# Forming the low halves of the split weights with an accumulating DMA instead of a VectorE subtraction

## The chip, the cores and the metric

The kernel runs on one core of a Trainium2 chip. The metric is the time of one execution on the device in microseconds (us); the times of a kernel are given as the median of several runs. Five engines work side by side, each through its own instructions in order: TensorE (PE, matrix products; PEld is its weight loads), VectorE (DVE), ScalarE (ACT), GpSimd (POOL) and SyncE (SP, which here only issues transfers). Sixteen DMA engines move data between the device memory (HBM) and the on-chip memory (SBUF); a transfer is issued by one of the engines' queues and is moved by all sixteen.

## The reference

Two decoder layers over a sequence of 512 positions with 1024 channels, in float32. Layer 0 mixes by windowed pooling and block-sparse attention, layer 1 by a gated recurrence (RG-LRU); each is followed by a gated feed-forward block with a short convolution.

```python
h = rms_norm(x, norm_mix[l])
x = x + (pool_attn_mixer(h, ...) if l % 2 == 0 else rglru_mixer(h, ...))
h = rms_norm(x, norm_ffn[l])
x = x + conv_ffn(h, ffn_w_in[l], ffn_conv_w[l], ffn_conv_b[l], ffn_w_out[l])
# rglru_mixer: z = h @ w_in; gate, xr = split(z); xr = causal_dwconv(xr)
# r, i = sigmoid of two 128x128 block products of xr;  a = exp(-8 r softplus(-lam))
# b = sqrt(1 - a^2) * (i * xr);  hs = scan(a, b);  out = (gelu(gate) * hs) @ w_out
```

All products are computed to nearly float32 precision. TensorE multiplies a rounded type (float32r), so each operand is split into a high part (rounded) and a low part (what the rounding left), and a product is three: high·high, high·low, low·high.

## The kernel before

Activations are kept with channels on the 128 partitions and the 512 positions along the free axis. The weights stream through in 218 chunks of up to 128x1024 float32 (512 KB), 99.1 MB in all, in the order in which TensorE uses them: 8 chunks of the query and key projections, 17 more of the first mixer, 76 of the first feed-forward block, 41 of the recurrence, 76 of the second feed-forward block. A feed-forward block is done in two halves of 22 up chunks (24 products of 512 columns each: the tiles `up`) and 16 down chunks (18 or 15 products: `dn`). The recurrence has 20 chunks of its input projection (`xr` for the branch, `gt` for the gate), 5 small chunks of 128x512 for the gate products (`gp`; each serves two of the ten blocks), then 16 down chunks.

A chunk passes three steps. SP loads it into a raw buffer (`wraw`, three of them, line 182). ACT rounds it into the high part (`whi`, line 195). DVE subtracts the high part from the raw one into the low part (`wlo`, line 196). The five gate chunks use their own buffers, `shi` and `slo`, of which there is one each; all others rotate through four pairs `whi`/`wlo`. `wnext` keeps three chunks converted ahead of the one in use, so chunk i takes the buffers of chunk i-4, and its conversion can begin when TensorE has read chunk i-4 for the last time. A gate chunk can be converted only when the products of the gate chunk before it are done.

`mm3` (lines 217 to 220) issues the three products in the order high·high, high·low of the activation, low·high: the low part of a chunk is first read by its third product (in the token projections, where the weights are the moving operand, by the second).

A scheduler lays out each engine's instructions from the program and its dependences; in parts of the program (`pe["on"]`: the first mixer and the recurrence) TensorE's order is fixed by hand. In the recurrence, `RG_ORDER` lists the steps: branch tile (x), gate products (p), gate tile (g), exponentials (e), square roots (q), scan (s), gelu (o), product (y). A step s has three instructions in a chain: DVE forms `h` (line 770), POOL multiplies it by `yy` (line 771), DVE scans (line 772). The five scans of a batch come one after the other. POOL otherwise does little: the sums of squares `ss` of the norms (line 260), the window sums of the pooling, and the product `yy<-i,a` (line 813).

Of the kernel before, what the change touches and what calls it, by code (L numbers as in the profile page):

```python
# [14 lines left out]
ALU = mybir.AluOpType  # L15
# [23 lines left out]
    _n += _w  # L39
NPA = _n  # L40

# Order of the first mixer: u/f = pooled projection now / as filler between attention steps, c = centre a window sum,
# v = value projection, m = split a pooled tile, a = attention.
MIX_ORDER = "u3 c3 u2 v m m f1 f0 a".split()
# Fillers of the attention loop: u = next projection group, m = split, p = pooled product, o = output product.
FILL_ORDER = "uuuuuuuuuuuuuuuuupmmpopp"
POOL_ORDER = (3, 2, 1, 0)
FILL_RATES = [float(c) for c in "1.6 1.95 1.45".split()]
# [8 lines left out]
CENTRE_AT = 5  # L57
V_BANKS = ("mm", "mm", "s", "av")
WARM = 20
# Order of the RG-LRU: x = branch tile, p = its gate products, g = gate tile, e = exps, q = roots, s = scan, o = gelu,  # L60
# y = output tile.
RG_ORDER = []
_c = dict.fromkeys("xpgeqsoy", 0)
for _kind in "xxgxpxpqxpgpgpeqsxsxxsssopyooxpxypygpgpqesssoosygsogyyogoyyggooyy":
    RG_ORDER.append((_kind, _c[_kind]))
    _c[_kind] += 1
RAW, WB, AHEAD = 3, 4, 3


@with_exitstack  # L70
def tile_trunk(ctx: ExitStack, tc: tile.TileContext, xT, par, fpar, w_v, w_q, w_k, w_u, w_pool, w_po, w_ao,
               f0_in, f0_out, r_in, r_ax, r_out, f1_in, f1_out, out):
    nc = tc.nc
# [7 lines left out]
    def T(tag, dt=F32):  # L81
        return cur["tp"].tile([P, S], dt, name=tag, tag=tag, bufs=cur["bufs"][tag])

    def phase(name, **bufs):
        if "cm" in cur:
            cur["cm"].__exit__(None, None, None)
        cur["cm"] = tc.tile_pool(name=name, bufs=1)
        cur["tp"] = cur["cm"].__enter__()
        cur["bufs"] = bufs
# [23 lines left out]
    def f(t):  # L113
        return t.bitcast(F32)
# [20 lines left out]
    chunks = []  # L135
# [31 lines left out]
    ready = []  # L167
# [7 lines left out]
    def load(parts=1):  # L175
        src, n = chunks[len(raws)]
        raw = wp.tile([P, 1024], F32, name="wraw", bufs=RAW)[:, :n]
        for i in range(parts):
            c = slice(i * n // parts, (i + 1) * n // parts)
            nc.sync.dma_start(raw[:, c], src[:, c])  # L180
        raws.append(raw)

    def convert():
        n = chunks[len(ready)][1]
        if len(raws) == len(ready):
            load()
        raw = raws[len(ready)]
        if n == S and "shi" in cur["bufs"]:
            hi, lo = T("shi", F32R), T("slo", F32R)
        else:  # L190
            hi, lo = (wp.tile([P, 1024], F32R, name=t, bufs=WB)[:, :n] for t in ("whi", "wlo"))
        parts = 2 if len(ready) < 2 else 2 if pe["on"] and len(ready) in FINE else 1
        for i in range(parts):
            c = slice(i * n // parts, (i + 1) * n // parts)
            nc.scalar.copy(hi[:, c], raw[:, c])  # L195
            nc.vector.tensor_tensor(lo[:, c], raw[:, c], f(hi[:, c]), op=ALU.subtract)  # L196
        ready.append((hi, lo, n))

    def wnext(n, ahead=AHEAD):
        while len(ready) < min(used[0] + 1 + ahead, len(chunks)):  # L200
            convert()
        hi, lo, got = ready[used[0]]
        assert got == n
        used[0] += 1
        return hi, lo
# [109 lines left out]
            if len(spans) == 1:  # L315
                after(d)

# [1 line left out]
    phase("mix0", qka=20, pm=4, hn=5, bias=1, lg=4)  # L319
    psum("ps0", mm=3, s=2, tr=2, av=1)  # L320
    warm = onesr.bitcast(BF16)
# [356 lines left out]
        g()  # L678
    ring[:] = ["mm", "s", "mm", "s", "mm", "av"]

# [1 line left out]
    def ffn(layer, norm, after, cuts=None):  # L682
        def conv(m):
            c0 = (layer * 2 * NF + m) * 4
            cw = [fprm[:, c0 + i:c0 + i + 1] for i in range(4)]
            ps = up_tile(norm, "up")
            bc = norm.bc
            z = T("z")
            nc.vector.tensor_tensor(z, ps, bc, op=ALU.mult)  # L689
            a = T("a")  # L690
            nc.scalar.activation(a, z, AF.Identity, scale=cw[2], bias=cw[3])  # L691
            for sh, w in ((1, cw[1]), (2, cw[0])):
                nc.vector.scalar_tensor_tensor(a[:, sh:], z[:, :S - sh], w, a[:, sh:], op0=ALU.mult, op1=ALU.add)  # L693
            return a

        for h0 in range(2):
            half(h0 * NF // 2, conv, after if h0 else (lambda d: None), cuts if h0 else None)
# [17 lines left out]
    n1 = Norm("nm1")  # L715
    ffn(0, nf, n1.tile_done)

# [1 line left out]
    phase("mix1", z=2, a=3, xrs=6, i=2, h=10, gz=6, shi=1, slo=1, yy=20)  # L719
    lam = prm[:, PC["lam"]:PC["lam"] + RB]  # L720
    sc = [cst.tile([P, RB], F32, name=f"sc{i}") for i in range(5)]
# [19 lines left out]
    now = {"set": "", "last": None, "before": None, "conv": None}  # L741
# [10 lines left out]
    for kind, n in RG_ORDER:  # L752
# [29 lines left out]
        if kind == "x":  # L782
# [5 lines left out]
            a = T("a")  # L788
# [6 lines left out]
            hi, lo = T("xrs", F32R), T("xrs", F32R)  # L795
# [4 lines left out]
        a, xh, xl = XC[n]  # L800
# [3 lines left out]
        for s in range(2):  # L804
            c = slice((2 * (n % 2) + s) * P, (2 * (n % 2) + s + 1) * P)
            gp = PS("gp", "tr")
            mm3(gp, gwh[:, c], gwl[:, c], xh, xl, True, True)
            o = T("yy" if s == 0 else "i")
# [87 lines left out]
```

## Time and profile before

| | |
|---|---|
| median of 3 runs | 1108.43 us (1108.22 to 1109.06) |
| span of the profiled execution | 1106.8 us |
| PE busy | 1091.4 us, 99% |
| DVE busy | 726.8 us, 66% |
| ACT busy | 514.6 us, 46% |
| POOL busy | 89.7 us, 8% |
| DMA, mean | 95 GB/s |

The span runs from the first instruction to the last on the device; the median of the runs is 1.6 us longer than it. TensorE is busy nearly throughout, but matmuls overlap: each is shown with 389 ns, while one begins every 227 ns in a steady stretch, so a chunk of 24 products takes 5.44 us, and a busy share alone does not tell a stall. Stalls are read from the starts of the matmuls and from the bracket with the idle time in the timeline.

### The profile page before, as it was taken

The page shows a single profiled execution, that of the slowest core. Times are in us where ns is not written, and L with a number is a line of the kernel's source. Part 1 is how long each engine was busy: PE and PEld are TensorE (multiplying, and loading weights), DVE is VectorE, ACT ScalarE, POOL GpSimd, SP SyncE. Part 2 cuts the span into 40 slices and gives each one's busy share as a digit, 9 for nine tenths or more (in the row PEclk, how much of TensorE's full clock was granted, in tenths as well). Part 3 has the DMA queues.
Part 4 walks back from the last instruction along what each step waited for, and adds up shares of the span by engine and source line. Part 5 has one row for each costly group of instructions (what it writes and reads, how often), then busy time and mean ns, then how long its engine had stood idle before and what let it go on. Part 6 is the DMA issues. An engine that isn't in the chain of part 4 may idle for free.

```text
span 1106.8 us, 12775 instructions
## 1 busy us (share of the span) xinstructions
PE 1091.4 (99%) x4895; PEld 893.2 (81%) x4895; DVE 726.8 (66%) x1013; ACT 514.6 (46%) x749; POOL 89.7 (8%) x70
## 2 busy tenths in 40 slices
PE   8999999999999999999999899999999999999998
PEld 6887778888888888888888687788888888888887
DVE  7777867877753477764486979448777435777631
ACT  6556656544432344444458695444444323444320
POOL 4030002100000000000202323120000000000000
PEclk9999999999999999999999999999999999999999
DMA  6332112222223322223332131342322243332241
GB/s 223 129 95 87 58 39 71 102 95 96 72 82 111 117 96 98 94 73 91 113 113 105 48 101 48 99 136 95 102 97 78 79 119 116 96 95 84 72 137 51
DMA packets 35261, 105.40 MB, mean 95 GB/s; under 512 B 4096, under 2 KB 4992, under 8 KB 35200
## 3 DMA queue, kind: packets, MB, share of 16 engines
q1 hardware_dynamic: 34416, 103.48, 28.7%
q10 hardware_dynamic: 784, 1.11, 0.4%
q8 instruction: 38, 0.62, 0.2%
q14 instruction: 23, 0.19, 0.1%
HBM read 101.43 MB, written 2.10 MB: 94 GB/s over the span
## 4 chain that ended last, share of the span: by engine, by line
PE 90%; DVE 6%; ACT 2%; issue 1%; DMA 0%; POOL 0%; SPq 0%; DVEq 0%; POOLq 0%; ACTq 0%
PE up L218 43%; PE dn L218 26%; PE tk L218 5%; PE xr L218 2%; PE gt L218 2%; PE po L218 2%; PE u L218 2%; PE ao L218 2%; DVE h L772 1%; PE s L218 1%; DVE wlo L196 1%; PE tr L221 1%; PE gp L218 1%; DVE a L791 1%; DVE h L770 1%
## 5 line engine op out<-in xcount | busy, mean ns | idle before, releaser
L195 ACT CAST whi<-wraw 128x1024 fp32r<-128x1024 f32 (+3 forms) x225 | 202.5, 904 | 281.0 <-PE dn L218 154.2
L196 DVE TENSOR_TENSOR wlo<-wraw,whi 128x1024 fp32r<-128x1024 f32 (+3 forms) x225 | 238.9, 1065 | 114.2 <-ACT whi L195 111.6
L218 PE MATMUL up<-xl,whi 128*128 128x512 f32 x704 | 274.0, 389 | 0.0
L218 PE MATMUL up<-xh,whi 128*128 128x512 f32 x704 | 273.9, 389 | 0.0
L218 PE MATMUL up<-xh,wlo 128*128 128x512 f32 x704 | 273.9, 389 | 0.0
L218 PE MATMUL dn<-yy,whi 128*128 128x512 f32 (+1 forms) x886 | 269.2, 386 | 2.4 <-ACT yy L230 2.0
L218 PEld LDWEIGHTS dn<-yy,whi 128*128 128x128 f32 x886 | 165.8, 189 | 36.9 <-ACT yy L230 2.8
L218 PE MATMUL dn<-yy,wlo 128*128 128x512 f32 (+1 forms) x443 | 170.7, 385 | 0.0
L218 PEld LDWEIGHTS up<-xl,whi 128*128 128x128 f32 x704 | 132.2, 188 | 27.9 <-DVE xl L234 0.5
L218 PEld LDWEIGHTS up<-xh,whi 128*128 128x128 f32 x704 | 132.2, 188 | 27.4
L218 PEld LDWEIGHTS up<-xh,wlo 128*128 128x128 f32 x704 | 132.2, 188 | 27.2
L693 DVE SCALAR_TENSOR_TENSOR a<-z,fprm,a 128x510 f32<-128x510 f32 (+1 forms) x176 | 131.1, 748 | 4.2 <-ACT a L691 1.1
L689 DVE TENSOR_TENSOR z<-up,rbc 128x512 f32<-128x512 f32 x88 | 60.5, 688 | 89.1 <-PE up L218 89.1
L218 PEld LDWEIGHTS dn<-yy,wlo 128*128 128x128 f32 x443 | 83.6, 189 | 16.4
L260 POOL TENSOR_TENSOR ss<-ss,sq 128x512 f32<-128x512 f32 x28 | 41.3, 1475 | 494.1 <-ACT sq L259 493.6
L230 ACT CAST yy<-y 128x512 fp32r<-128x512 f32 x44 | 27.3, 621 | 112.1 <-DVE y L707 112.1
L312 DVE TENSOR_TENSOR x<-dn,x 128x512 f32<-128x512 f32 (+1 forms) x41 | 27.8, 679 | 73.9 <-PE dn L218 73.9
L691 ACT ACTIVATE a<-z,fprm 128x512 f32<-128x512 f32 x88 | 71.4, 814 | 3.8 <-DVE z L689 3.2
L704 ACT ACTIVATE gg<-a 128x512 f32<-128x512 f32 x44 | 27.8, 632 | 81.1 <-DVE a L693 81.0
L231 DVE TENSOR_TENSOR yy<-y,yy 128x512 fp32r<-128x512 f32 x44 | 30.5, 692 | 28.9 <-ACT yy L230 28.9
L218 PE MATMUL tk<-wlo,xh 128*128 128x512 f32 x96 | 37.7, 392 | 1.9 <-DVE wlo L196 1.9
L218 PE MATMUL tk<-whi,xh 128*128 128x512 f32 x96 | 37.9, 400 | 1.2 <-ACT whi L195 1.2
(177 smaller groups left out, 1229.5 us busy)
## 6 DMA issues: line engine op xcount, KB each, us to landing
wraw<-in_dram SPq DMA_DIRECT2D x131, 512.0 KB, 3.3
wraw<-in_dram SPq DMA_DIRECT2D x48, 320.0 KB, 2.8
wraw<-in_dram SPq DMA_DIRECT2D x32, 384.0 KB, 3.0
x<-in_dram SPq DMA_DIRECT2D x8, 256.0 KB, 5.9
out_dram<-x SPq DMA_DIRECT2D x7, 256.0 KB, 2.0
wraw<-in_dram SPq DMA_DIRECT2D x6, 256.0 KB, 2.7
qka<-qka ACTq DMA_DIRECT2D x8, 128.0 KB, 2.6
wraw<-in_dram SPq DMA_DIRECT2D x4, 128.0 KB, 3.8
```

The costliest lines, as they stand in the source:

```text
L195: nc.scalar.copy(hi[:, c], raw[:, c])
L196: nc.vector.tensor_tensor(lo[:, c], raw[:, c], f(hi[:, c]), op=ALU.subtract)
L218: in_order(nc.tensor.matmul(*a, **k))
L221: in_order(nc.tensor.transpose(*a))
L230: nc.scalar.copy(hi, src)
L231: nc.vector.tensor_sub(lo, src, f(hi))
L260: nc.gpsimd.tensor_tensor(self.ss, self.ss, sq, op=ALU.add)
L312: nc.vector.tensor_tensor(X[d][:, t], ps[:, t], X[d][:, t], op=ALU.add)
L689: nc.vector.tensor_tensor(z, ps, bc, op=ALU.mult)
L691: nc.scalar.activation(a, z, AF.Identity, scale=cw[2], bias=cw[3])
L693: nc.vector.scalar_tensor_tensor(a[:, sh:], z[:, :S - sh], w, a[:, sh:], op0=ALU.mult, op1=ALU.add)
L704: nc.scalar.activation(gg, g, AF.Gelu_apprx_tanh)
```

## The change

From the ninth chunk on (`BY_DMA = 8`) the low part is formed in two steps. ACT writes the negated high part into the low buffer, and POOL issues a DMA that reads the weights a second time from HBM and adds them onto it. The raw buffer is then read by ACT alone. The first eight chunks stay as they were. Ten chunks of the first mixer that were converted in two halves are converted in one piece. The rest of the diff takes out comments, which shifts line numbers by up to 8 (the chunk conversion of before and of after both stand near line 195).

```diff
+BY_DMA = 8
@@ def convert():
             hi, lo = (wp.tile([P, 1024], F32R, name=t, bufs=WB)[:, :n] for t in ("whi", "wlo"))
+        if len(ready) >= BY_DMA:
+            nc.scalar.copy(hi, raw)
+            nc.scalar.mul(lo, f(hi), -1.0)
+            nc.gpsimd.dma_start(out=lo, in_=chunks[len(ready)][0], accum_op=ALU.add)
+            ready.append((hi, lo, n))
+            return
         parts = 2 if len(ready) < 2 else 2 if pe["on"] and len(ready) in FINE else 1
```

TensorE's order does not change. POOL gets 210 DMAs among its other work. Before, this is POOL's order through the two halves of the recurrence, from the sums of squares to the second batch of scan products (line 813 is the product `yy<-i,a`, line 771 the scan product `h`):

```order
26 L260 TENSOR_TENSOR ss<-ss,sq 128x512 x14
27 L813 TENSOR_TENSOR yy<-i,a 128x512 x5
28 L771 TENSOR_TENSOR h<-h,yy 128x512 x5
29 L813 TENSOR_TENSOR yy<-i,a 128x512 x5
30 L771 TENSOR_TENSOR h<-h,yy 128x512 x5
```

Nothing but elementwise work stands there. After, the second half of the same place, from the end of the first batch on, reads (lines 821 and 779 are the same two products):

```order
96 L197 DMA wlo<-in_dram 128x1024 x2
97 L197 DMA slo<-in_dram 128x512
98 L821 TENSOR_TENSOR yy<-i,a 128x512 x2
99 L197 DMA wlo<-in_dram 128x1024
100 L197 DMA slo<-in_dram 128x512
101 L821 TENSOR_TENSOR yy<-i,a 128x512
102 L197 DMA wlo<-in_dram 128x1024 x2
103 L821 TENSOR_TENSOR yy<-i,a 128x512
104 L197 DMA wlo<-in_dram 128x1024
105 L821 TENSOR_TENSOR yy<-i,a 128x512
106 L779 TENSOR_TENSOR h<-h,yy 128x512 x5
107 L197 DMA wlo<-in_dram 128x1024 x2
```

The two DMAs of row 107 belong to the last two chunks of the gate projection, the ninth and tenth `gt` tiles; they now stand behind the five products of the second batch.

On ACT, before, the same place is the end of the recurrence's gate products (`yy`, `i` and `h` are the sigmoids and the tanh of a block, then come the roots of `h`, the exponentials of `yy` and the gelus of `gz`):

```order
465 L195 CAST whi<-wraw 128x1024
466 L809 ACTIVATE yy<-gp,prm 128x512
467 L809 ACTIVATE i<-gp,prm 128x512
468 L815 ACTIVATE h<-yy,c_4671 128x512
469 L765 ACT_TABLE_LOAD
470 L765 ACTIVATE h<-h 128x512 x5
471 L760 ACT_TABLE_LOAD
472 L760 ACTIVATE yy<-yy,c_4670 128x512 x5
473 L775 ACT_TABLE_LOAD
474 L775 ACTIVATE gz<-gz 128x512 x3
475 L195 CAST whi<-wraw 128x1024
```

After:

```order
582 L195 CAST whi<-wraw 128x1024 x2
583 L196 ACTIVATE wlo<-whi 128x1024
584 L817 ACTIVATE yy<-gp,prm 128x512
585 L817 ACTIVATE i<-gp,prm 128x512
586 L823 ACTIVATE h<-yy,c_4747 128x512
587 L773 ACT_TABLE_LOAD
588 L773 ACTIVATE h<-h 128x512 x5
589 L768 ACT_TABLE_LOAD
590 L768 ACTIVATE yy<-yy,c_4746 128x512 x5
591 L783 ACT_TABLE_LOAD
592 L783 ACTIVATE gz<-gz 128x512 x2
593 L196 ACTIVATE wlo<-whi 128x1024
```

The negation of the ninth `gt` chunk (row 593) stands behind the roots, the exponentials and two gelus, while its rounding (the second of row 582) stands ahead of them.

At each gate chunk one more ACT instruction and one DMA come between the rounding and the product. The fifth gate chunk after:

```order
564 L195 CAST whi<-wraw 128x1024
565 L195 CAST shi<-wraw 128x512
566 L196 ACTIVATE wlo<-whi 128x1024
567 L196 ACTIVATE slo<-shi 128x512
568 L797 ACTIVATE a<-z,prm 128x512
```

The negation of the big chunk beside it stands ahead of that of the gate chunk, and so does its DMA on POOL (rows 99 and 100 above).

## Rows read from the trace of the kernel before

**Rows 1.** The page's part 1: engine, busy us (share of the span), instructions.

```profile
span 1106.8 us, 12775 instructions
PE 1091.4 (99%) x4895; PEld 893.2 (81%) x4895; DVE 726.8 (66%) x1013; ACT 514.6 (46%) x749; POOL 89.7 (8%) x70
```

**Rows 2.** Chain that ended last, shares of the span by engine (page, part 4).

```profile
PE 90%; DVE 6%; ACT 2%; issue 1%; DMA 0%; POOL 0%; SPq 0%; DVEq 0%; POOLq 0%; ACTq 0%
```

**Rows 3.** Windows: stretch, length, busy PE, PEld, DVE, ACT, POOL, clock, DMA share, GB/s.

```profile
91.00:174.00 83.00, 82.45 (x424) 61.70 (x424) 62.77 (x155) 53.67 (x135) 3.77 (x3) 1.00 0.15 52
374.00:494.00 120.00, 120.00 (x532) 99.38 (x531) 84.22 (x107) 52.09 (x65) 0.00 (x0) 1.00 0.28 92
600.00:645.00 45.00, 41.17 (x173) 32.98 (x172) 37.08 (x42) 31.92 (x43) 14.05 (x9) 0.96 0.17 58
645.00:694.00 49.00, 45.33 (x196) 36.22 (x195) 40.80 (x48) 32.97 (x49) 14.18 (x8) 1.00 0.29 90
864.00:924.00 60.00, 60.00 (x266) 49.71 (x265) 23.14 (x29) 14.82 (x19) 0.00 (x0) 1.00 0.36 106
```

**Rows 4.** Groups (page, part 5): count, then busy us, mean ns, idle time before.

```profile
L196 DVE TENSOR_TENSOR wlo<-wraw,whi 128x1024 fp32r<-128x1024 f32 (+3 forms) x225 | 238.9, 1065 | 114.2 <-ACT whi L195 111.6
```

**Rows 5.** Chain in time order, start us, us: 22 up, 16 down chunks.

```profile
374.00 119.68 PE up L218 x528
...
863.95 59.84 PE dn L218 x264
```

**Rows 6.** DMA queues (packets, MB, share of 16 engines) and issues (us to landing).

```profile
q1 hardware_dynamic: 34416, 103.48, 28.7%
q10 hardware_dynamic: 784, 1.11, 0.4%
...
wraw<-in_dram SPq DMA_DIRECT2D x131, 512.0 KB, 3.3
...
wraw<-in_dram SPq DMA_DIRECT2D x6, 256.0 KB, 2.7
```

**Rows 7.** Timeline (start us, us): gate chunks 2 to 5, rounding, first low product.

```profile
584.76 0.61 ACT L195 CAST shi<-wraw 128x512 fp32r<-128x512 f32 x1
...
589.67 0.39 PE L218 MATMUL gp<-xrs,slo 128*128 128x512 f32 x1
...
597.60 0.62 ACT L195 CAST shi<-wraw 128x512 fp32r<-128x512 f32 x1
...
603.27 0.39 PE L218 MATMUL gp<-xrs,slo 128*128 128x512 f32 x1
...
626.63 0.61 ACT L195 CAST shi<-wraw 128x512 fp32r<-128x512 f32 x1
...
633.59 0.39 PE L218 MATMUL gp<-xrs,slo 128*128 128x512 f32 x1
...
644.13 0.60 ACT L195 CAST shi<-wraw 128x512 fp32r<-128x512 f32 x1
...
647.68 0.39 PE L218 MATMUL gp<-xrs,slo 128*128 128x512 f32 x1
```

**Rows 8.** Timeline: ninth gt chunk rounded, first low product; last POOL scan product.

```profile
654.00 1.06 ACT L195 CAST whi<-wraw 128x1024 fp32r<-128x1024 f32 x1 [1.00 <-PE gt L218]
...
672.16 0.39 PE L218 MATMUL gt<-xh,wlo 128*128 128x512 f32 x1
...
674.07 2.07 POOL L771 TENSOR_TENSOR h<-h,yy 128x512 f32<-128x512 f32 x1 [0.70 <-DVE h L770]
```

**Rows 9.** Timeline: TensorE's stalls in the recurrence; window: its clock after one.

```profile
623.84 0.49 PE L218 MATMUL gp<-xrs,shi 128*128 128x512 f32 x1 [3.18 <-ACT xrs L796]
...
679.00 0.50 PE L218 MATMUL gt<-xh,wlo 128*128 128x512 f32 x1 [1.24 <-DVE wlo L196]
...
693.10 0.50 PE L218 MATMUL dn<-yy,whi 128*128 128x512 f32 x1 [1.98 <-ACT yy L230]
...
625.90:629.30 3.40, 3.40 (x10) 2.62 (x9) 3.40 (x5) 2.08 (x5) 0.00 (x0) 0.51 0.08 31
```

## The prediction

> **What bounds the kernel now.** I read the page's busy table first: TensorE is busy 99% of 1106.8 us, VectorE 66%, ScalarE 46% [rows 1]. The chain that ended last confirms it: 90% of it is TensorE, 6% VectorE [rows 2]. So taking work from VectorE can pay only where VectorE stands in the chain. The windows show where that is: in the feed-forward stages TensorE is busy without a hole (120.00 of 120.00 us, 60.00 of 60.00), in the attention stretch it misses 0.55 us of 83, and in the recurrence between 600 and 694 us it misses 3.83 and 3.67 us [rows 3]. A gain of any size must come from those 94 us.
>
> **What is removed.** Of the 225 subtractions (1.065 us each on average, 238.9 us) [rows 4] and five on the gate chunks, only the first eight chunks keep theirs: 220 instructions and some 231 us leave VectorE. In the feed-forward stages this is worth nothing, since nobody waits for it there. In the recurrence TensorE has three stalls. The first, before 623.84, waits for the rounding of a branch tile (3.18 us); no subtraction of a weight is behind it, and I leave it. The second, before 679.00, waits for a weight's low part that VectorE formed late (1.24 us idle, 1.4 us by the starts). The third, before 693.10, waits for the output tiles, behind VectorE's queue (1.98 us idle, 2.1 by the starts). After the first the granted clock stood at 0.51 for 3.4 us, the lower of its two levels (1.2 GHz), which costs 1.7 us [rows 9]. I count the same behind the third, of like length, and nothing behind the shorter second. If both of the later stalls go, that is 1.4 + 2.1 + 1.7 = **5.2 us saved**, the most that relief of VectorE can bring there.
>
> **What is added, and its cover.** ScalarE gets 210 negations. None is in the trace; I price them as the rounding of the same size, 1.06 us for a full chunk [rows 8] and 0.61 for a gate chunk [rows 7], some 197 us in all, which takes ScalarE from 46% to some 64%. In an up stage it is busy 52 of 120 us and gets 22 x 1.06 = 23 more: there is room.
>
> The DMA has no row. Below it lies the load of the same bytes: 3.3 us from issue to landing for 512 KB, 2.7 for 256 KB, issue included [rows 6]. Since it must fetch what it adds to, a second read comes on top. From below that is nothing; from beside, another load: 28.7% of the engines' span for 103.48 MB is 3.07 us per MB, 1.6 us for 512 KB; from above, a copy from SBUF to SBUF, whose queue took 0.4% for 1.11 MB, 4.0 us per MB, 2.1 us [rows 6]. I take 1.6, the nearer since an accumulation writes once: **4.9 us** to landing. I take it for gate chunks too, because their DMA now stands behind that of a full chunk on POOL. The issue on POOL is bounded by nothing (it is in the 3.3) and by the longest single POOL instruction shown, 2.07 us [rows 8]; I take 1.5.
>
> The Trainium skill (Collectives: The Full Stack, section on the bandwidth ceiling) says that an add in the DMA path costs no time for the adding, but two source reads where a copy has one, so that it runs at half the copy's rate. By it the landing would also be 3.3 + 1.6 us and the sum unchanged; a single read would take 1.6 us off every stall below. No run so far shows an accumulating DMA.
>
> For the steady stages this is covered. A chunk lasts 119.68 / 22 = 5.44 us in an up stage, 59.84 / 16 = 3.74 in a down stage [rows 5], and its buffers come free three chunks ahead of its use: 16.3 and 11.2 us. The path is 1.06 + 1.06 + 1.5 + 4.9 = 8.5 us, less for the smaller down chunks. Without that cover each chunk would stall. The engines' share: 210 of 218 chunks are 94.9 of 99.1 MB; one read more is 26.3% of the span, two 52.6%. With the loads' 28.7% that is 81%. SP's order stays, and it gets its raw buffers back earlier, as ScalarE alone reads them. On POOL the sums of squares now stand among DMAs that wait for ScalarE; they are due only after the first up chunk (5.44 us), and I count nothing for them.
>
> **The gate chunks.** They have one buffer pair, so the cover is not three chunks but whatever lies between two products. From the rounding's start to the first low product there are now 4.91, 5.67, 6.96 and 3.55 us for the second to fifth [rows 7]; the first has far more. The new path is 0.61 + 0.61 + 1.5 + 4.9 = 7.6 us. It is late by 2.7, 2.0, 0.7 and 4.1: **9.5 us**. With a landing of 2.7 us and a free issue it is late by 0.4 us in all; with 5.4 and 2.07 (path 8.7), by 13.7.
>
> **The ninth gt chunk.** Its DMA stands on POOL behind the five scan products, and its negation on ScalarE behind roots and exponentials. The last scan product ends at 674.07 + 2.07 = 676.14, and TensorE reads this low part at 672.16 [rows 8]. The scans' chain has no subtraction of a weight in it, so I leave its end where it is. Late by 676.14 + 1.5 + 4.9 - 672.16 = **10.4 us** (7.3 to 11.5). Behind it TensorE's last products wait, and the scans and output tiles catch up meanwhile, which is why I let both later stalls go.
>
> **The clock.** This stall and the two longest gate stalls, each longer than 2.1 us, bring 3.4 us at half clock: 3 x 1.7 = **5.1 us**.
>
> **Sum.** 9.5 + 10.4 + 5.1 - 5.2 = 19.8 us. The span becomes 1126.6; the median stood 1.6 us above the span, so **1128 us**. By the lower bounds it is 0.4 + 7.3 + 1.7 - 5.2 = +4.2 us, 1113. By the upper ones 13.7 + 11.5 + 6.8 - 5.2 = +27, and a down stage, whose share is 0.36 already [rows 3], would be full: total 28.7 + 0.4 + 94.9 x 0.64% = 90% of the span, 90 / 29.1 x 0.36 = 1.1, so 10% on four stages of 60 us, +24 more: 1159.
>
> **Rivals.**
> *The DMA engines become the bound.* If an accumulated byte costs three loads instead of two, the engines need 29.1 + 3 x 26.3 = 108% of the span, 1195 us, and with the recurrence's stalls some 1210; at four loads 134%, 1490. For it: no row shows the adding, and the loads' share is 0.28 to 0.36 in the stages that make up most of the time. Against it: the loads' share contains waiting for each other, so the engines have more left than it says. Its sign would be TensorE waiting for a DMA in every feed-forward stage. 0.14.
>
> *Faster.* Place: the ninth gt chunk. If the second batch of scan products ended early enough for its DMA to be in time, the relief of 5.2 us would remain and the kernel would come to 1104. With my prices the gate chunks alone (9.5) outweigh the relief, so it also needs landings like a plain load's, with a free issue (0.4 late). Then it decides at 5.2 - 0.4 - 1.7 = 3.1 us of lateness of the ninth gt chunk: the batch must end by 672 instead of 676.14. For it: VectorE has fewer instructions around the batch. Against it: the batch follows the exponentials, and no subtraction lies inside it. 0.06.
>
> *No change.* The same, half way: 0.04.
>
> *Descriptors starve.* POOL could be kept from writing them while VectorE works, so that each issue takes up to a VectorE instruction longer, 1.07 us [rows 4]: gate chunks 4 x 1.07 and the ninth gt chunk 1.07 later, +5.4, 1134. VectorE is busy 84 of 120 us in an up stage [rows 3], but has less to do after. The Trainium skill (SBUF — State Buffer, the box on DMAs blocked by VectorE) describes this block, for VectorE's modes that use two ports for one operand; here most VectorE work has two tensor inputs. Not seen in any run so far. 0.04.
>
> **How the numbers follow.** The forecast has 0.72. Only the faster rival is below 1106.2; within 0.2%, about what a measurement of this kernel tells from no change, lies 0.04; slower are 0.72 + 0.14 + 0.04 = 0.90. For 8 times in 10 the range runs from 1110, just under the lower bounds, to 1185, which adds to the upper bounds' 1159 the mild cases of a DMA bound; left out are the faster and unchanged cases and most of that rival.
>
> **What would show it.** In the profile after: VectorE near 500 us and ScalarE near 710; up and down stages as long as before; TensorE waiting in the recurrence for DMAs into `slo` (2 to 4 us, up to four times) and once some 10 us for `wlo` in the ninth `gt` tile, after POOL's fifth `h`; half clock behind the long ones. It is wrong if feed-forward stages grow, if the accumulated DMA lands in 3 us or in 8, or if the scans end much earlier.

## The result, and the profile after

The changed kernel takes 1127.53 us (median of four runs, 1123.76 to 1129.56) against 1108.45 us (1108.22 to 1109.06) for the kernel before: 1.0166 times as long, 95% interval 1.0146 to 1.0185, or 18.4 us more by the ratio. The forecast was 1128. The profiled run took 1129.56 us with a span of 1127.3 us, 20.5 us longer than the span before. Three executions in the runs below, one of them of the kernel before, ran at a mean granted clock of 0.556 to 0.656 and took 1553.25 to 1821.6 us; the ratios leave them out.

Busy times of the kernel after (page, part 1: busy us, share of the span, instructions), against [rows 1]:

```profile
PE 1095.3 (97%) x4895; PEld 896.1 (79%) x4895; DVE 513.3 (46%) x793; ACT 691.8 (61%) x949; POOL 261.8 (23%) x280
```

VectorE lost 213.5 us and ScalarE gained 177.2. TensorE did the same 4895 products and was busy 3.9 us longer, which I put down to its clock (0.988 in the mean here); its idle time rose from 15.4 to 32.0 us, and that is where the rest went: 16.6 + 3.9 = 20.5 us.

What the added instructions cost (after, groups of instructions by line: count, busy us, mean ns of one; lines have moved by eight), beside the subtraction of [rows 4]:

```profile
L196 ACT ACTIVATE wlo<-whi 128x1024 fp32r<-128x1024 f32 (+2 forms) x205 | 193.0, 942 | 3.0
L197 POOL DMA_DIRECT2D wlo<-in_dram x205 | 176.5, 861 | 754.7 <-ACT wlo L196 719.3 <-DVE hn L377 18.0 <-PE s L226 11.8
```

The DMA engines (after: queues with packets, MB and share of 16 engines; below them issues with KB and median us from issue to landing), against [rows 6]:

```profile
q0 software_dynamic: 30240, 94.91, 51.3%
q1 hardware_dynamic: 34416, 103.48, 26.9%
...
wraw<-in_dram SPq DMA_DIRECT2D x131, 512.0 KB, 4.2
wlo<-in_dram POOLq DMA_DIRECT2D x124, 512.0 KB, 5.5
...
slo<-in_dram POOLq DMA_DIRECT2D x5, 256.0 KB, 6.8
```

The added queue moves fewer bytes than the loads' queue and takes nearly twice its share. The loads themselves land later than before, 4.2 us for 3.3.

Where it matters is a question for the stages. The windows of after (stretch, length, busy PE, PEld, DVE, ACT, POOL, clock, DMA share, GB/s): an up stage, a down stage and the two halves of the recurrence, against [rows 3]:

```profile
384.00:504.00 120.00, 120.00 (x531) 99.40 (x530) 62.24 (x87) 72.26 (x91) 19.63 (x23) 1.00 0.83 182
884.00:944.00 60.00, 60.00 (x266) 49.71 (x265) 8.42 (x12) 27.88 (x34) 13.82 (x16) 1.00 0.90 197
600.00:645.00 45.00, 37.06 (x151) 29.11 (x150) 29.10 (x34) 36.12 (x47) 18.60 (x16) 0.92 0.56 124
645.00:700.00 55.00, 41.51 (x159) 33.28 (x158) 28.62 (x33) 37.33 (x54) 20.79 (x17) 0.82 0.58 127
```

With the DMA engines busy for 83 and 90% of it, the feed-forward stages still have TensorE at work without a hole. The recurrence has lost: in its two halves TensorE is without work for 7.94 and 13.49 us, and works part of the rest at half clock.

What TensorE waited for in the kernel after (waits: us in all, times, the longest):

```profile
PE gt L226 <- DMA wlo<-in_dram: 9.8, 1, 9.8
PE gp L226 <- DMA slo<-in_dram: 8.8, 4, 3.7
PE gp L226 <- ACT xrs L804: 3.2, 1, 3.2
...
PE up L226 <- DMA wlo<-in_dram: 1.6, 1, 1.6
```

The first two rows are new and hold 18.6 us: one low part of the ninth gt chunk, and four low parts of gate chunks. The third stood in the kernel before too. The last is new as well, a chunk of the second feed-forward block. The two later stalls of [rows 9], before 679.00 and 693.10, are gone.

The timeline of after around the last gate chunk and the ninth gt chunk (start us, us, engine, line, operation; in brackets the idle time before and what ended it):

```profile
647.96 1.06 ACT L196 ACTIVATE wlo<-whi 128x1024 fp32r<-128x1024 f32 x1
...
648.92 0.61 ACT L196 ACTIVATE slo<-shi 128x512 fp32r<-128x512 f32 x1
649.32 0.87 POOL L197 DMA_DIRECT2D wlo<-in_dram  x1 [5.19 <-ACT wlo L196]
...
650.10 0.98 POOL L197 DMA_DIRECT2D slo<-in_dram  x1
...
657.21 0.79 PE L226 MATMUL gp<-xrs,slo 128*128 128x512 f32 x1 [3.69 <-DMA slo<-in_dram]
...
680.92 1.04 ACT L196 ACTIVATE wlo<-whi 128x1024 fp32r<-128x1024 f32 x1
...
687.16 2.05 POOL L779 TENSOR_TENSOR h<-h,yy 128x512 f32<-128x512 f32 x1 [0.69 <-DVE h L778]
...
689.15 0.87 POOL L197 DMA_DIRECT2D wlo<-in_dram  x1
...
694.39 0.79 PE L226 MATMUL gt<-xh,wlo 128*128 128x512 f32 x1 [9.80 <-DMA wlo<-in_dram]
```

The gate chunk's negation and DMA each stand right behind those of a full chunk, and its product starts 7.1 us after the issue. The ninth gt chunk is negated at 680.92, but its DMA starts only when GpSimd is done with the fifth scan product (687.16 + 2.05), 4.6 us after TensorE wanted the low part (694.39 - 9.80 = 684.59).

### The profile page after: what moved, and what is told of

Same layout as the page of the kernel before. It is cut to its first block, busy times and chain, and to the rows that moved or that the text cites. A ratio compares the mean times of both kernels' runs of the same rounds, so it can differ in the third digit from the quotient of the medians.

```text
span 1127.3 us, 13240 instructions
## 1 busy us (share of the span) xinstructions
PE 1095.3 (97%) x4895; PEld 896.1 (79%) x4895; DVE 513.3 (46%) x793; ACT 691.8 (61%) x949; POOL 261.8 (23%) x280
## 3 DMA queue, kind: packets, MB, share of 16 engines
q0 software_dynamic: 30240, 94.91, 51.3%
q1 hardware_dynamic: 34416, 103.48, 26.9%
## 4 chain that ended last, share of the span: by engine, by line
PE 87%; DMA 4%; issue 3%; ACT 2%; DVE 2%; POOL 1%; SPq 0%; POOLq 0%; ACTq 0%; DVEq 0%
PE up L226 42%; PE dn L226 25%; PE tk L226 5%; PE gt L226 2%; PE u L226 2%; PE po L226 2%; PE xr L226 2%; PE ao L226 2%; DMA slo<-in_dram 2%; PE s L226 1%; DMA wlo<-in_dram 1%; PE tr L229 1%; PE av L226 1%; DVE h L780 1%; DMA wraw<-in_dram 1%
## 5 line engine op out<-in xcount | busy, mean ns | idle before, releaser
L197 POOL DMA_DIRECT2D wlo<-in_dram x205 | 176.5, 861 | 754.7 <-ACT wlo L196 719.3
L195 ACT CAST whi<-wraw 128x1024 fp32r<-128x1024 f32 (+2 forms) x205 | 192.9, 941 | 244.2 <-PE dn L226 126.7
L196 ACT ACTIVATE wlo<-whi 128x1024 fp32r<-128x1024 f32 (+2 forms) x205 | 193.0, 942 | 3.0
L701 DVE SCALAR_TENSOR_TENSOR a<-z,fprm,a 128x511 f32<-128x511 f32 (+1 forms) x176 | 132.0, 750 | 84.1 <-ACT a L699 80.8
L268 POOL TENSOR_TENSOR ss<-ss,sq 128x512 f32<-128x512 f32 x28 | 39.0, 1393 | 33.2 <-ACT sq L267 31.4
L226 PE MATMUL gt<-xh,wlo 128*128 128x512 f32 x80 | 33.2, 414 | 9.8 <-DMA wlo<-in_dram 9.8
```

The lines of the kernel that those rows point to most:

```text
L195: nc.scalar.copy(hi, raw)
L196: nc.scalar.mul(lo, f(hi), -1.0)
L197: nc.gpsimd.dma_start(out=lo, in_=chunks[len(ready)][0], accum_op=ALU.add)
L226: in_order(nc.tensor.matmul(*a, **k))
L268: nc.gpsimd.tensor_tensor(self.ss, self.ss, sq, op=ALU.add)
```

## The experiments

The theory to test was the prediction's: five low parts arrive late, because the path to them has become longer than its cover, and everything else is free. Against it stood that the added traffic slows the kernel generally, that ScalarE's negations delay the recurrence, and, for the ninth gt chunk, that not its place in GpSimd's queue but the transfer makes it late. All ratios below are to the kernel before, run on the same chip; a difference of two kernels in us is that of their ratios times 1108.45.

### Where the 18 us are: one part at a time

**The feed-forward blocks alone.** All chunks of the attention part, the recurrence and its output projection keep the subtraction.

```
-        if len(ready) >= BY_DMA:
+        if 25 <= len(ready) < 101 or len(ready) >= 142:
```

> One part of the change alone: the negation and the accumulating DMA for the chunks of the two feed-forward blocks only; all chunks of the recurrence and its output projection go by subtraction on VectorE, as before. Some three quarters of the added traffic is left. Lateness theory: the feed-forward blocks keep TensorE busy throughout at 83 to 90% of the DMA engines' time, so 1108 us, 1106 to 1111; the small stall at the start of the second block (1.6 us) may stay. Traffic theory: three quarters of the 19 us stay, about 1122. Negation theory: the recurrence is as before, 1108.

Measured 1109.06 us, ratio 1.0000 (0.9991 to 1.0009). 152 of the 210 DMAs and negations cost nothing that shows beside an interval of 1 us. This is against the traffic theory, which had 1122.

**Gate chunks by subtraction**, the other 205 by DMA.

```
+        gate = n == S and "shi" in cur["bufs"]
...
-        if len(ready) >= BY_DMA:
+        if len(ready) >= BY_DMA and not gate:
```

> One part undone: the five gate chunks in the single buffer pair shi/slo go back to the subtraction on VectorE; the other 205 low parts still come by the accumulating DMA. Lateness theory: the four stalls of 1.83, 1.27, 2.47 and 3.85 us before gp<-xrs,slo (9.4 in all) go, and one or two of the half-clock stretches that follow them with it (2 to 4 us); the stall before the ninth gt chunk (9.8) stays. About 1115 us, 1111 to 1118. Traffic theory (200 MB of added DMA slow the kernel everywhere): five of 210 transfers are nothing, 1127. Negation theory (ScalarE's added work delays the recurrence): 5 of 210 negations go, 1125 to 1127.

Measured 1117.32 us, ratio 1.0079 (1.0066 to 1.0092): 9.6 us of the 18.4 came from five chunks of 210. No product waits for `slo` any more, and the ninth gt chunk's 9.5 us stay.

**The ninth gt chunk converted ahead of the batch.** At the second batch's roots one chunk is converted in advance, so that its negation stands ahead of them on ScalarE, and its DMA ahead of the five products on GpSimd.

```
         if kind == "q":
+            while len(HS) == RB and len(ready) <= used[0] + AHEAD:
+                convert()
```

> One thing moved: at the second batch of the recurrence the next weight chunk (the ninth gt chunk) is converted ahead of the roots on ScalarE and, its DMA, ahead of the five scan products on GpSimd, and not behind them; nothing is left out. Lateness theory: the stall of 9.8 us before gt<-xh,wlo at 694 goes, with the half-clock stretch of 13.7 us around it shortened to what it was before (3 to 5 us back); the four gate stalls (9.4) stay. About 1114 us, 1111 to 1119. If it is the transfer's own time and not its place in GpSimd's queue that makes it late, the stall stays above 5 us and the time above 1120. Traffic theory: 1127.

Measured 1125.26 us, ratio 1.0144 (1.0128 to 1.0161). Only 2.4 us came back where 10 and more were expected. The timeline of this kernel shows why:

```profile
669.42 1.05 ACT L196 ACTIVATE wlo<-whi 128x1024 fp32r<-128x1024 f32 x1
...
670.78 0.88 POOL L197 DMA_DIRECT2D wlo<-in_dram  x1 [0.48 <-ACT wlo L196]
...
690.90 1.05 ACT L196 ACTIVATE wlo<-whi 128x1024 fp32r<-128x1024 f32 x1
...
692.24 0.88 POOL L197 DMA_DIRECT2D wlo<-in_dram  x1 [3.57 <-ACT wlo L196]
...
697.43 0.80 PE L226 MATMUL gt<-xh,wlo 128*128 128x512 f32 x1 [7.91 <-DMA wlo<-in_dram]
```

The ninth chunk is now in time: negated at 669.42, issued at 670.78, no wait. So its place in the queue was what made it late, and not its transfer. But the tenth takes over: its negation now stands on ScalarE behind a gated cast that waits for the scan batch, at 690.90, and its low part is 7.91 us late. **Both edits together** (gate chunks by subtraction, ninth chunk early):

> Both of the edits: gate chunks by subtraction on VectorE, the ninth gt chunk converted ahead of the scan's batch. Lateness theory: all five stalls go, and the two stalls that the change removed (1.4 and 2.1 us, with a clock stretch of 1.7) stay gone: 1103 to 1109 us, about 1105, that is a little under the kernel before (1108.4). Traffic theory: 1125 or more. Negation theory: some 1115 to 1125, with no stall that a low part ends but TensorE waiting for ScalarE in the recurrence.

Measured 1116.59 us, ratio 1.0068 (1.0055 to 1.0081), 1.2 us from the run with the gate chunks alone; the tenth chunk waits 7.9 us here as well. Both expectations missed by the same step: I had followed one chunk through the queues, and not the next one.

**The last two gt chunks by subtraction too.**

```
-        if len(ready) >= BY_DMA and not gate:
+        if len(ready) >= BY_DMA and not gate and len(ready) not in (124, 125):
```

> Low parts by subtraction on VectorE for the five gate chunks and the last two gt chunks (the ninth and the tenth, whose conversion falls behind the second scan batch), by the accumulating DMA for the other 203. Put from the run with both edits, in which the tenth gt chunk came 7.9 us late in place of the ninth because its negation stood on ScalarE behind a cast that waits for the scan batch. Theory as now put (the two added steps, negation and DMA, both stand behind the scan batch's chain on in-order engines, the subtraction on VectorE does not): the stall of 9.5 us and its half-clock stretch go, 1117.3 - 9.5 - 2 = 1105.8 us, 1103 to 1109. If the last chunks are late for a reason that has nothing to do with the added steps, a stall over 4 us stays there: 1112 or more.

Measured 1111.53 us, ratio 1.0026 (1.0017 to 1.0035): 5.9 us less than with the gate chunks alone. That is less than the stall of 9.5 that goes, because other waits come up where TensorE now arrives earlier (waits of this kernel):

```profile
PE dn L227 <- DMA wlo<-in_dram: 2.3, 1, 2.3
PE gt L227 <- DVE wlo L205: 1.9, 1, 1.9
...
PE gt L227 <- DMA wlo<-in_dram: 1.6, 1, 1.6
```

Two of them are low parts by DMA again, of the output projection's first chunk and of the fifth gt chunk. **So these go by subtraction too**, with the rest of the output projection (17 chunks; 186 DMAs and negations are left):

```
-        if len(ready) >= BY_DMA and not gate and len(ready) not in (124, 125):
+        if len(ready) >= BY_DMA and not gate and len(ready) not in (120, 124, 125) and not 126 <= len(ready) < 142:
```

> As the run with the gate chunks and the last two gt chunks by subtraction, and besides them the fifth gt chunk and the recurrence's output chunks: 17 more of 203 low parts off the DMA. Put to close the account of the 2.6 us that were left there. Theory: the stall of 1.6 us at the fifth gt chunk and that of 2.3 at the output's first low part are low parts that land late too; without them 1108 to 1110 us, no more than 1 us from the kernel before. If a general cost of the added traffic or of the negations is left, 1111 or more.

Measured 1109.12 us, ratio 1.0002 (0.9993 to 1.0011), and the account is closed: 9.6 us in the gate chunks, 5.9 in the last two gt chunks, 2.7 in the fifth gt chunk and the output projection, 0.2 left, within the interval. So the loss lies in 24 of 210 conversions at the most; of the output projection's 16 only the first was seen late. With 186 negations on ScalarE and 86.78 MB of accumulating DMA still in the kernel, no general cost of the traffic or of the negations above 1 us is left.

### Does relief of VectorE bring anything?

The same kernel answers a part of this. Its page (part 1) and its waits:

```profile
PE 1092.0 (99%) x4895; PEld 894.0 (81%) x4895; DVE 532.0 (48%) x817; ACT 675.5 (61%) x925; POOL 241.7 (22%) x256
```

```profile
PE dn L227 <- ACT yy L239: 2.0, 1, 2.0
...
PE gt L227 <- DVE wlo L205: 0.8, 1, 0.8
```

VectorE has 195 us less to do than in the kernel before, and the stalls of [rows 9] stand there again: 2.0 us as in the kernel before, 0.8 for 1.24. So relief elsewhere brings nothing that shows. Just ahead of these two stalls, though, this kernel has no relief: the last two gt chunks and the output projection are subtracted on VectorE as before, and VectorE does the same 24 instructions there without a gap (windows, the kernel before first: length, busy PE, PEld, DVE, ...). Four of the 24 are subtractions of weights, 3.6 us together.

```profile
669.46:688.96 19.50, 18.26 (x81) 14.81 (x80) 19.50 (x24) 6.76 (x11) 5.29 (x3) 1.00 0.17 51
669.63:689.15 19.52, 18.69 (x83) 15.16 (x82) 19.52 (x24) 6.75 (x11) 5.31 (x3) 1.00 0.18 51
```

In the kernel with the last two gt chunks by subtraction but the output projection by DMA (1111.53 us), three of the four are gone. Timelines, the kernel before (the first and the last of the four, then the cast that makes the last output tile's high part), then that kernel (the last scan, then the same cast):

```profile
677.75 1.19 DVE L196 TENSOR_TENSOR wlo<-wraw,whi 128x1024 fp32r<-128x1024 f32 x1
...
687.55 0.81 DVE L196 TENSOR_TENSOR wlo<-wraw,whi 128x640 fp32r<-128x640 f32 x1
...
692.43 0.62 ACT L230 CAST yy<-gz 128x512 fp32r<-128x512 f32 x1 [0.76 <-DVE gz L779]
```

```profile
680.33 1.21 DVE L781 TENSOR_TENSOR_SCAN h<-yy,h 128x512 f32<-128x512 f32 x1
...
694.75 0.62 ACT L239 CAST yy<-gz 128x512 fp32r<-128x512 f32 x1 [0.76 <-DVE gz L788]
```

In the kernel before, the last scan ends at 677.83 and the cast at 693.05, 15.2 us later, and so it is in the kernel with 186 DMAs. With three subtractions fewer it is 13.8 us. So the subtractions do lengthen the way to the output tiles, by 1.4 us here. That kernel could not turn it into time, since the first output chunk's low part came 2.3 us late by its DMA.

To test it from the other side, **one chunk alone** goes by DMA: the tenth gt chunk, whose subtraction in the kernel before stands on VectorE behind the second scan batch. It is written so that its DMA stands after two of the batch's five products; a second kernel has the same order without the DMA.

```
-for _kind in "xxgxpxpqxpgpgpeqsxsxxsssopyooxpxypygpgpqesssoosygsogyyogoyyggooyy":
+for _kind in "xxgxpxpqxpgpgpeqsxsxxsssopyooxpxypygpgpqessgsoosysogyyogoyyggooyy":
...
-        if len(ready) >= BY_DMA:
+        if len(ready) == 125:
...
+            if n == 7:
+                convert()
...
-            nc.gpsimd.tensor_tensor(h, h, BB[n], op=ALU.mult)
+            behind(nc.gpsimd.tensor_tensor(h, h, BB[n], op=ALU.mult), now["dma"])
```

> The accumulating DMA for one chunk alone, the tenth gt chunk, whose subtraction in the kernel before stands on VectorE behind the second scan batch (678.94 us, the low product waits 1.24). Its conversion is written ahead of the third scan step of that batch, the negation ahead of the first gated cast on ScalarE and the DMA after two of GpSimd's five scan products. Relief theory (the prediction's: a low part that leaves VectorE takes the stalls of 1.4 and 2.1 us and a half-clock stretch of 1.7 with it): 1103 to 1106 us, under the kernel before (1108.5). Place theory (the stalls at 679 and 693 follow from the scan batch and not from VectorE's subtractions, and a DMA issued at 671 lands about when the subtraction ended): 1107 to 1110, with the stall at 693 left.

> The control of the kernel with one chunk by DMA: the same writing order and conversion ahead, with all low parts by subtraction on VectorE. Both theories: 1106 to 1110 us; what the one DMA brings is the difference of the two, 3 to 5 us by the relief theory and within 1.5 by the place theory.

Measured 1108.43 us, ratio 0.9999 (0.9990 to 1.0008), with the DMA, and 1109.20 us, ratio 1.0005 (0.9997 to 1.0014), without. The timelines, first with the DMA, then the control, show TensorE's longest wait at the recurrence's end:

```profile
693.44 0.80 PE L227 MATMUL dn<-yy,whi 128*128 128x512 f32 x1 [1.96 <-ACT yy L792]
```

```profile
693.34 0.80 PE L227 MATMUL dn<-yy,whi 128*128 128x512 f32 x1 [2.02 <-ACT yy L792]
```

In both, the stall at the tenth gt chunk is gone, in the control with its subtraction still on VectorE, so the order alone removes it. In both, TensorE comes earlier to the output projection and waits there for the output tiles, until 693.44 and 693.34, where the kernel before waited until 693.10. Taking this one low part off VectorE moves a stall; what it brings is within the noise, and not the 3 to 5 us of the relief theory. The pair is no clean price of 1.2 us of VectorE's work, since with the DMA the last scan ends 1.3 us later than in the control (681.63 for 680.36), for a reason that was not tried. The end of the recurrence is set by the chain of the scan batch through the gating to the output tiles, and on VectorE the output projection's subtractions stand among the links of that chain in both kernels. What it would bring to have these low parts made elsewhere and in time was not tried.

### What the addition costs, and the single pair

**The same DMA without the addition.**

```
-            nc.gpsimd.dma_start(out=lo, in_=chunks[len(ready)][0], accum_op=ALU.add)
+            nc.gpsimd.dma_start(out=lo, in_=chunks[len(ready)][0])
```

> The same DMA on the same queue without the addition: it overwrites the negated high part with the weights, so the low part is left unsummed (the addition is what is left out), and the destination is not read. It prices the addition: if the second read makes the landing longer by the 1.6 us that the sum took, the four gate stalls shrink by some 6 us and the stall at the ninth gt chunk by some 2, with a half-clock stretch or two fewer: about 1118 us, 1114 to 1121; DMA engines some 25 points less busy than 83% in the attention's stretch. If the addition costs nothing in the landing, 1126 to 1128.

Measured 1117.85 us, ratio 1.0080 (1.0066 to 1.0094): half of the loss is the addition's. Issues of this kernel (KB, us to landing), and below them its GpSimd queue:

```profile
wlo<-in_dram POOLq DMA_DIRECT2D x124, 512.0 KB, 4.2
...
slo<-in_dram POOLq DMA_DIRECT2D x5, 256.0 KB, 4.4
```

```profile
q0 software_dynamic: 30240, 94.91, 30.0%
```

The addition makes the landing, issue included, 1.3 us longer for a full chunk (5.5 for 4.2) and 2.4 for a gate chunk (6.8 for 4.4). The issue itself takes 0.53 us of GpSimd's time without it and 0.86 with it. The engines' time becomes 1.7 times as long (51.3% for 30.0%; in the up stage the engines are 0.60 busy, not 0.83). The gate stalls shrink from 8.8 us (four) to 4.0 (three), and that of the ninth gt chunk from 9.8 to 8.2, which is near the 1.6 us that the prediction gave the second read.

**Gate chunks in the four rotating pairs**, with the DMA.

```
-    phase("mix1", z=2, a=3, xrs=6, i=2, h=10, gz=6, shi=1, slo=1, yy=20)
+    phase("mix1", z=2, a=3, xrs=6, i=2, h=10, gz=6, yy=20)
```

> The gate chunks take the four rotating buffer pairs in place of their own single pair, with the accumulating DMA kept for all: they can be converted up to three chunks ahead. If the gate stalls come from the single pair (a chunk's DMA can start only when the one before has been read to its end), the four stalls before gp<-xrs,slo shrink from 9.4 us to under 3, and the time is 1116 to 1122 us, with the stall of 9.8 at the ninth gt chunk left or up to 5 longer, since 25 chunks now share the four pairs. If the transfer is simply too slow for gate chunks wherever it starts, 1126 or more.

Measured 1126.08 us, ratio 1.0151 (1.0135 to 1.0166), 1.7 us less than the changed kernel and above the range I gave. Its waits:

```profile
PE gt L226 <- DMA wlo<-in_dram: 16.8, 4, 12.7
PE gp L226 <- ACT xrs L804: 5.5, 1, 5.5
```

No product waits for a gate chunk's low part any more, so the single pair was what made those late. But the gt chunks, whose pairs they now share, wait 16.8 us for 9.8. I had allowed 5 us more there; it was 7, and 2.3 at a branch tile that I had not seen coming.

### The negation without the DMA

**ScalarE negates, VectorE adds the loaded chunk in SBUF**, for all 210 chunks, and then the same with the last two gt chunks by plain subtraction.

```
-            nc.gpsimd.dma_start(out=lo, in_=chunks[len(ready)][0], accum_op=ALU.add)
+            nc.vector.tensor_tensor(lo, raw, f(lo), op=ALU.add)
```

> The negation is left on ScalarE for all 210 chunks, and the loaded weights are added to it by VectorE in SBUF, not by a DMA: the sums and the 193 us of negations stay, 95 MB of DMA and 210 issues on GpSimd go. Theory as now put: the gate chunks are on time again (no issue, no landing), the ninth gt chunk's negation stands ahead of the scan's end (at 681 in the changed kernel, its low product due at 684), but the tenth's stands behind the cast that waits for the batch and is some 2 to 4 us late: 1110 to 1114 us. If all the lateness is the DMA's, 1108. If ScalarE's added work is the whole of it, 1125 or more.

> The kernel with negations on ScalarE and the additions on VectorE (1123.1 us), with the last two gt chunks by plain subtraction. If its 14 us came from where the negation and the addition stand in the queues behind the scan batch, the 7.8 us stall and one half-clock stretch go: 1112 to 1116, with the wait of 7.7 us for xrs at the first batch left. If ScalarE's added 193 us cost a little everywhere, 1120 or more.

Measured 1123.08 us, ratio 1.0128 (1.0114 to 1.0142), and 1120.93 us, ratio 1.0112 (1.0099 to 1.0126). The first lies outside every range that I gave, the second outside that of the theory I held. The longest wait of the first:

```profile
PE gt L226 <- DVE wlo L197: 7.8, 1, 7.8
```

Two things can be read. No product waits for a gate chunk's low part, so their lateness was the DMA's. And the ninth gt chunk is late without any DMA: its addition waits for a negation at the place that the change gave it, and then stands behind the scan batch on VectorE, as the DMA did on GpSimd. What I had not expected is the wait of 7.7 us at the first batch (3.2 in the changed kernel), which stays in the second run; there the tenth gt chunk, subtracted on VectorE behind the scan batch, also waits 3.5 us, so the stall of 7.8 us shrank and did not go. In the first run's timeline an addition stands ahead of VectorE's work on the branch tile that TensorE waits for (from 629.20 on):

```profile
627.06 2.21 DVE L197 TENSOR_TENSOR wlo<-wraw,wlo 128x1024 fp32r<-128x1024 f32 x1
...
633.68 0.79 PE L226 MATMUL gp<-xrs,shi 128*128 128x512 f32 x1 [7.71 <-ACT xrs L804]
```

So these two kernels make additions on VectorE wait for negations on ScalarE, which the changed kernel doesn't do, and they are no measure of the negation by itself. That the second came out where I had put "ScalarE's work costs a little everywhere" does not make that theory right: the kernel with 186 negations at a ratio of 1.0002 speaks against it. How the 12 us split between the negations' places and the additions' was not tried.

## Why the prediction was right, point by point

**Only the recurrence can move.** Right but for a wait of 1.6 us at the start of the second feed-forward block. TensorE has no other hole that shows in the feed-forward stages, and with their 152 DMAs alone the time does not change measurably.

**The gate chunks, 9.5 us.** Right in size: 8.8 us of waits, four of them, and 9.6 us when undone, some half-clock time included. The terms behind it were off both ways, so that the sum came out well has some luck in it. From the issue on I had 1.5 + 4.9 = 6.4 us for each; the second to fifth took 4.6, 4.5, 6.8 and 7.1. I had assumed that each stands behind a full chunk's DMA. The fourth and fifth were issued 3.6 and 0.8 us after the DMA before them, the second and third 5.2 and 9.9 us after it (timeline, the second):

```profile
585.66 0.85 POOL L197 DMA_DIRECT2D slo<-in_dram  x1 [4.27 <-DVE a L799]
...
590.24 0.50 PE L226 MATMUL gp<-xrs,slo 128*128 128x512 f32 x1 [1.68 <-DMA slo<-in_dram]
```

They were late by 1.7, 1.1, 2.3 and 3.7 us where I had 2.7, 2.0, 0.7 and 4.1. The issue itself is 0.86 us, not 1.5.

**The ninth gt chunk, 10.4 us.** Right as a stall (9.8), for the reason given: the DMA behind the fifth scan product. The batch ended 4.6 us after the low part was due (4.0 forecast), and 5.2 us passed from there to the product (6.4 forecast). What the prediction did not see is that the tenth chunk would be 7.9 us late if the ninth were not, and that the fifth gt chunk and the output projection's first are late by 1.4 to 2.3 us as soon as TensorE comes early enough to notice. It also missed the wait of 1.6 us before 764.34, at the start of the second feed-forward block; that low part was issued at 755.15 and took 9.1 us to land, so that its path, from the rounding at 752.73 on, was 11.6 us where I had 8.5.

**The relief of VectorE, -5.2 us.** The two stalls went from the changed kernel, but not by relief. The reason is the one given under the ninth gt chunk: TensorE comes some 10 us later to the same place, and VectorE has caught up by then (it waits 4.24 us for TensorE's last gate tile, until 702.51). A longer stall covers them, so the term did no harm in this sum. As a gain of its own, "the most that relief of VectorE can bring", no run shows it. The stall before 679.00 goes by the order alone, with the subtraction still on VectorE. Undoing the last two chunks gave back 5.9 us, not 10 and a stretch of clock, because the covered stalls or others like them came up again. For the stall before 693.10 the reading holds in part, since three subtractions fewer bring the last output tile 1.4 us closer to the scans; no kernel here turned that into time.

**The clock.** Net 3.4 us were forecast (5.1 less 1.7), and TensorE was busy 3.9 us longer. The stretches were not three of 3.4 us. The windows of after (length, busy PE, ..., clock):

```profile
625.30:632.10 6.80, 4.77 (x10) 3.43 (x11) 6.07 (x9) 6.71 (x9) 1.74 (x2) 0.50 0.46 86
656.00:662.80 6.80, 5.59 (x13) 4.43 (x14) 0.00 (x0) 4.41 (x6) 3.06 (x3) 0.50 0.93 229
686.70:700.40 13.70, 6.01 (x14) 4.75 (x15) 10.96 (x15) 8.25 (x13) 5.44 (x5) 0.50 0.69 143
```

The stretch behind the third stall of the kernel before, counted without a row, is there in its trace (694.20 to 697.60 at 0.50). In the kernel after, four were to be there, the three and that of [rows 9]; there are three, longer, and more than half of the longest lies inside the stall, where it costs nothing. The gate stalls were to bring two and brought one: that of 3.7 us has 5.6 us at half clock behind it, that of 2.3 us none (the clock was 1.00 from 637 to 645). That the net came out near is luck in part.

**The rivals.** The DMA engines did not become the bound of the kernel: 78.8% of the span over all queues (81 forecast), and up to 0.90 in a down stage with TensorE busy throughout. In one place they came to it: between 735 and 770 us, at the start of the second feed-forward block, their share was 0.96 to 1.05, and the low part that landed after 9.1 us lies there. With the feed-forward blocks alone by DMA the share reached 1.05 at this start too, and TensorE did not wait. Per MB the accumulating queue took 51.3 / 94.91 against the loads' 26.9 / 103.48, 2.1 times as much. The rule quoted from the Trainium skill (Collectives: The Full Stack, section on the bandwidth ceiling), two source reads and so half the copy's rate, agrees with that; on one and the same queue the price was a little less, 1.7 times. The descriptors did not starve: an issue took 0.86 us in the mean beside a VectorE that was busy 46% of the time, so nothing of the block that the Trainium skill describes (SBUF — State Buffer) was seen beside VectorE's two-input work. The faster rival lived on the relief of 5.2 us, which no run shows, and no kernel here came out below the kernel before by more than the noise.

**In the sum** the three terms that I had (9.5, 10.4 and the clock) come to 18.6 us of waits and 3.9 of clock, less 3.2 us of stalls covered, 19.3; with the 1.6 us before 764.34 that is 20.9. The span grew by 20.5 us, 19.8 forecast.

## What to carry to other kernels

Moving work off an engine with 66% of the time busy brought nothing, because nearly all of that work lay where nobody waits for it; look at what ends a wait, at what else stands on that engine ahead of it, and at whether the next wait is ready behind it. A step that is cut in two and spread over two more in-order queues needs its cover checked at every place where those queues wait for something else, and for each chunk after the first late one; here 24 of 210 places held all of the loss. A stall that disappears behind a longer one has not been gained.

## What the runs showed of the hardware

The same wait can bring different lengths of half clock. In the kernel before, the wait of 3.18 us before 623.84 was followed by 3.4 us at 0.51 from 625.90 on [rows 9]; the control kernel of the one-chunk test has the same wait to the hundredth, and its clock is at half already before the product that ends it, for 6.7 us (timeline, then window):

```profile
623.97 0.80 PE L227 MATMUL gp<-xrs,shi 128*128 128x512 f32 x1 [3.18 <-ACT xrs L809]
```

```profile
623.30:630.00 6.70, 5.85 (x13) 4.33 (x14) 6.70 (x9) 5.47 (x9) 0.00 (x0) 0.50 0.15 39
```

Runs of one kernel differ in this too. The longest and the shortest of the four runs of the changed kernel (spans 1127.3 and 1121.8 us) had mean granted clocks of 0.988 and 0.994. Long stalls alone do not make a time less sharp: the four runs of the kernel with waits of 7.7 and 7.8 us lie 1.1 us apart, and 27 runs of the kernel before 4.1.

An accumulating DMA landed later in the changed kernel when another had been issued just ahead of it. With 256 KB it took 4.5 and 4.6 us from the issue to the product that waited for it where the DMA before it on GpSimd was issued 9.9 and 5.2 us earlier, and 6.8 and 7.1 us where that was 3.6 and 0.8 us. So the median of 6.8 for 256 KB against 5.5 for 512 KB does not mean that a smaller one is slower.
